# Three pairs of neighbouring RWKV stages, each issued as one, in a hybrid RWKV-7 / attention block

## The chip, the cores and the metric

The kernel runs on one core of a Trainium2 chip. The metric is the device time of one execution in microseconds; the time before is the median of three runs. The work is spread over TensorE (PE, with its weight loads shown as PEld), VectorE (DVE), ScalarE (ACT), GpSimd (POOL) and SyncE (SP), which issues the transfers.

## The reference

One decoder block in fp32: 16 learned meta tokens are put ahead of 256 tokens, a projection feeds two branches (RWKV-7 time mixing and an attention with forget gates, "FoX"; 16 heads of 64 each), a gated merge joins them, and a SwiGLU network follows. The part that the change touches is the time mixing:

```python
def step(S, inp):
    r_t, w_t, k_t, v_t, a_t, b_t = inp
    sa = jnp.einsum('bhvk,bhk->bhv', S, a_t)
    S = (S * w_t[:, :, None, :] + sa[..., None] * b_t[:, :, None, :]
         + v_t[..., None] * k_t[:, :, None, :])
    return S, jnp.einsum('bhvk,bhk->bhv', S, r_t)
...
y = _wkv7_scan(rh, dh, kh, vh, -kk, kk * ah)
y = (y - mu) * lax.rsqrt(var + GN_EPS)
y = y * gn_w + gn_b
y = y + jnp.sum(rh * kh * r_k, axis=-1, keepdims=True) * vh
```

## The kernel before

**Weights.** Each product with a weight matrix is made of three TensorE passes: the weight tile `raw` comes by a transfer, ACT casts its high part `wh` (L336), DVE subtracts to get the low part `wl` (L337), and TensorE multiplies high by high, high by low and low by high (L347 to L349; L423 and L425 where the two activations stand side by side). raw, wh and wl have four buffers each, so ACT and DVE run at most four tiles ahead of TensorE.

**Groups.** The 16 heads are worked in four groups g of four heads. For each group TensorE runs jobs over weight tiles: RWKV k, v and r, two low-rank products, FoX q, k and v (with f for the attention's k), and behind groups 0 to 2 two gate jobs (zg). Behind group 3 come nine more gate jobs, then the branch products, the output product and the SwiGLU network.

**Background streams.** What is not a weight product is a generator: `rwkv_bg` for time mixing and `fox_bg` for attention. It issues one stage and yields a number, in ns of a virtual clock, after which the next stage may come. The jobs call `slot` after every k-tile, which moves the virtual clock on and issues the stages that are due. The order of TensorE is what this gives at build time, and TensorE works strictly down that list. The other engines' order is chosen by a scheduler from the same program. The names Y_* are the yielded numbers.

**The time mixing of one group**, in stages of `rwkv_bg`: norms and decays (to Y_AB); first tables, m = 0, then second tables, m = 1 (L782 to L787: 16 small fp32 matmuls `mat` each by L373, evicted into NK by DVE L786); the meta block's tables (8 matmuls, DVE L795) with the transfers d1 and ln; bonus bs (L829); two transposes trbk of the bk tables (L842, ACT L843); the values' transposes trv (ACT L852); the meta block's transposes tr0 (ACT L859 and L861). Then DVE eliminates in 31 steps (lt L874, lx L876), in 112 lanes. The result goes through DRAM into X and X0 by 13 transfers of SP (d2 L881, d3 L883, X L887, X0 L888). After a yield of LANE = 24000 the chain begins: XT is transposed on DVE (L953) while TensorE makes rhs of the meta block, then QT (32 tiny matmuls, evicted by ACT L962), X12 (evicted by ACT L970), four scan steps (rhs, u, y, s), a group norm on DVE (L979 to L988, its reciprocal root in L263 to L272) and the transposes yT back to channel order (L996, put into ya by L999 to L1005). A group's chain runs while TensorE does the next group's jobs, so a group's norm and its yT fall among the next group's tables. FoX stages wait in `slot` for a chain stage to share a place with, as far as the four small PSUM banks allow.

Words used below: a main matmul is one of L347 to L349; an island is a run of small matmuls between two main ones; sc are FoX's scores, fss and fk its norms' sums.

Of the kernel before, what the change touches and what calls it, by code (L numbers as in the profile page):

```python
# [81 lines left out]
Y_KK = 2900  # L82
Y_DECAY = 1400
Y_AB = 6000
Y_MAT = 2900
Y_NEXT = 2300
Y_BONUS = 1200
Y_TRBK = 1400
Y_TRV = 1100
Y_TR0 = 1600  # L90
Y_RHS = 1400
Y_U = 1400
Y_XT = 1400
# [7 lines left out]
def hybrid_block(ctx, tc, A, out, dbg=None):  # L101
# [18 lines left out]
    def aux_ps(name):  # L120
        return psa.tile([P, 512], F32, tag="aux", name=name)
# [249 lines left out]
    def pe_mm(out_, lhsT, rhs, start, stop, skip=False):  # L371
        clock[2] += 4 * max(lhsT.shape[-1], rhs.free_size()) / 2.4
        nc.tensor.matmul(out_, lhsT, rhs, start=start, stop=stop, skip_group_check=skip)  # L373

    def pe_tr(out_, in_, ident_):
        clock[2] += P / 2.4
        nc.tensor.transpose(out_, in_, ident_)
# [278 lines left out]
    def rwkv_jobs(g):  # L656
# [24 lines left out]
        def mul(w):  # L681
            (uh, ul), (gh, gl) = w
            gg = box["gg"] = ot(f"gg{g}")
            for m in range(2):
                ms = slice(m * P, (m + 1) * P)
                ps = main_ps(f"g{g}{m}")[:, :T]
                for k in range(2):
                    mm3(ps, gh[:, k, ms], gl[:, k, ms], sgh[:, k, :], sgl[:, k, :], k == 0, k == 1)
                nc.vector.tensor_copy(gg[:, m, :], ps)
            with tc.manual_schedule(engines={nc.scalar.engine}):  # L690
                for nm, i, dh, dl, bname in (("sig", 0, twh, twl, "w0"), ("aa", 1, adh, adl, "a0")):
                    dst = box[nm] = et(f"{nm}{g}")
                    for m in range(2):
                        ms = slice(m * P, (m + 1) * P)
                        ps = (aux_ps if i == 0 else main_ps)(f"{nm}{g}{m}")[:, :L]
                        mm3(ps, uh[:, i, ms], ul[:, i, ms], dh, dl, True, True)
                        nc.scalar.activation(dst[:, m, :], ps, AF.Sigmoid, bias=vc(bname, 2 * g + m))

                nc.scalar.preload_act_table_set("natural_log_exp_and_others")
            spawn(rwkv_bg(g, box), HOP)  # L700
# [3 lines left out]
    def hb(h):  # L704
        return slice(h * HD, (h + 1) * HD)

    def tok(c):

        return slice(0, HD) if c < 0 else slice(NMETA + c * HD, NMETA + (c + 1) * HD)

    def bcast(ap, n):
        return ap.unsqueeze(1).to_broadcast([P, n, ap.shape[1]])

    def rwkv_bg(g, box):
# [64 lines left out]
        for m in range(2):  # L779
            pss = [aux_ps(f"mat{g}{m}{h}") for h in range(2)]  # L780
            for c in range(4):
                for h in range(2):  # L782
                    pe_mm(pss[h][:, c * P:(c + 1) * P], bk[hb(h), m, c].rearrange("p x t -> p (x t)"),
                                     ar[hb(h), :, m, tok(c)], start=True, stop=True)
            for h in range(2):
                nc.vector.tensor_tensor(NK[:, h, 4 * m:4 * m + 4, :], pss[h].rearrange("p (c w) -> p c w", w=P),  # L786
                                        bcast(mup, 4), op=ALU.mult)  # L787
            yield Y_MAT
        pss = [aux_ps(f"mat0{g}{h}") for h in range(2)]
        for m in range(2):  # L790
            for h in range(2):
# [47 lines left out]
        for m in range(2):  # L839
            ps = aux_ps(f"trbk{g}{m}")  # L840
            for c in range(4):
                pe_tr(ps[:, c * P:(c + 1) * P], bkf[:, 4 * m + c, :], ident)  # L842
            nc.scalar.activation(BK[:, :, 4 * m:4 * m + 4, :].rearrange("p h c d -> p c h d"),  # L843
                                 ps.rearrange("p (c h d) -> p c h d", h=2, d=HD), AF.Copy)
            yield Y_TRBK
        ps = aux_ps(f"trv{g}")
        for m in range(2):
            for e in range(2):
# [2 lines left out]
        for cc in range(2):  # L851
            nc.scalar.activation(SV[HD:, :, cc::2, :].rearrange("p h i d -> p i h d"),  # L852
                                 ps[hb(cc), :].rearrange("p (i h d) -> p i h d", h=2, d=HD), AF.Copy)
        yield Y_TRV
        ps = aux_ps(f"tr0{g}")
        for m in range(2):
            pe_tr(ps[:, m * P:(m + 1) * P], bk0[:, m].rearrange("p x t -> p (x t)"), ident)
# [4 lines left out]
                             ps[:NMETA, 2 * P:].rearrange("p (m h d) -> p m h d", h=2, d=HD), AF.Copy)  # L862
        yield Y_TR0

# [578 lines left out]
```

## Time and profile before

| | us |
|---|---|
| runs | 1537.67, 1539.15, 1539.01 (median 1539.01) |
| profiled execution | 1540.85 |
| its span, mean granted clock | 1539.1, 0.999 |
| PE busy | 1529.6 (99%) |
| DVE busy | 1030.4 (67%) |
| ACT busy | 778.2 (51%) |
| POOL busy | 106.8 (7%) |
| waits of PE in the trace | 0.2 to 2.0 in an entry, six entries |

The groups' time mixing and attention lie in about the first 560 us of the span; the rest is gates, branches and the SwiGLU network. Busy shares over the whole span mix these, so the stages around one group's elimination are read in windows of their own. Times in timeline rows are from the span's start.

### The profile page before, as it was taken

What the parts mean: (1) busy time and instruction counts of PE and PEld (TensorE: products, weight loads), DVE (VectorE), ACT (ScalarE), POOL (GpSimd) and SP (SyncE); (2) the same over time, 40 slices, a digit from 0 to 9 for tenths busy, and PEclk for the clock granted to TensorE, in tenths of its full rate; (3) what the DMA queues carried; (4) which work ended last, traced back from release to release, by engine and by line L of the source; (5) the groups of instructions that cost most, each with busy time, mean ns of one, the idle gap of its engine ahead of it and who ended that gap; (6) DMA issues with size and microseconds to landing.
All of it is one profiled execution on the core that took longest, in us unless ns stands there. A gap on an engine that the chain in (4) does not pass through costs nothing.

```text
span 1539.1 us, 25987 instructions
## 1 busy us (share of the span) xinstructions
PE 1529.6 (99%) x10113; PEld 1352.5 (88%) x10113; DVE 1030.4 (67%) x1859; ACT 778.2 (51%) x1174; POOL 106.8 (7%) x186
## 2 busy tenths in 40 slices
PE   9999999999999999999999999999999999999998
PEld 9999899989989888998888888888888888888887
DVE  7887698688788857876565566666556666444443
ACT  7654465475465445554455455445445544333332
POOL 2111203302202000000000000000000000000000
PEclk9999999999999999999999999999999999999999
DMA  8566546546645757777566666666666665566663
GB/s 269 163 171 185 148 134 188 163 119 188 175 125 154 212 155 218 230 226 240 181 180 185 192 185 186 191 192 182 189 191 191 182 190 189 191 204 204 189 203 104
DMA packets 211483, 283.32 MB, mean 184 GB/s; under 512 B 23888, under 2 KB 128352, under 8 KB 211360
## 3 DMA queue, kind: packets, MB, share of 16 engines
q1 hardware_dynamic: 206752, 277.53, 60.7%
q10 hardware_dynamic: 4608, 4.13, 0.8%
q8 instruction: 79, 1.29, 0.3%
q14 instruction: 44, 0.36, 0.1%
HBM read 274.43 MB, written 7.19 MB: 183 GB/s over the span
## 4 chain that ended last, share of the span: by engine, by line
PE 95%; DVE 2%; ACT 1%; DMA 1%; SPq 1%; issue 1%; DVEq 0%; ACTq 0%
PE up L423 11%; PE gt L423 10%; PE zg L423 8%; PE dn L1306 5%; PE dn L1305 5%; PE dn L1304 5%; PE up L425 5%; PE gt L425 5%; PE zg L425 4%; PE f L347 2%; PE f L349 2%; PE f L348 2%; PE br L347 2%; PE f L423 2%; PE br L348 2%; PE br L349 2%
## 5 line engine op out<-in xcount | busy, mean ns | idle before, releaser
L337 DVE TENSOR_TENSOR wl<-raw,wh 128x1024 fp32r<-128x1024 f32 (+1 forms) x376 | 456.7, 1216 | 264.0 <-ACT wh L336 263.4
L336 ACT ACTIVATE wh<-raw 128x1024 fp32r<-128x1024 f32 (+1 forms) x376 | 393.9, 1049 | 424.8 <-PE up L423 117.5
L318 DVE TENSOR_TENSOR wl<-raw,wh 128x1024 fp32r<-128x1024 f32 x120 | 147.0, 1225 | 162.8 <-ACT wh L317 162.7
L423 PE MATMUL gt<-hts,wh 128*128 128x512 f32 x704 | 245.0, 394 | 0.0
L423 PE MATMUL up<-hts,wh 128*128 128x512 f32 x704 | 244.9, 394 | 0.0
L317 ACT ACTIVATE wh<-raw 128x1024 fp32r<-128x1024 f32 x120 | 127.0, 1058 | 194.4 <-PE dn L1305 141.5
L425 PE MATMUL gt<-hts,wl 128*128 128x256 f32 x660 | 186.2, 282 | 0.0
L425 PE MATMUL up<-hts,wl 128*128 128x256 f32 x660 | 186.0, 282 | 0.0
L423 PE MATMUL zg<-xhl,wh 128*128 128x512 f32 x512 | 182.4, 401 | 0.0
L423 PEld LDWEIGHTS up<-hts,wh 128*128 128x128 f32 x704 | 130.1, 188 | 26.5
L423 PEld LDWEIGHTS gt<-hts,wh 128*128 128x128 f32 x704 | 130.1, 188 | 26.5
L1305 PE MATMUL dn<-wh,acl 128*128 128x512 f32 x352 | 138.7, 394 | 0.0
L1306 PE MATMUL dn<-wl,ach 128*128 128x512 f32 x352 | 138.3, 393 | 0.0
L1304 PE MATMUL dn<-wh,ach 128*128 128x512 f32 x352 | 138.1, 392 | 0.0
L425 PE MATMUL zg<-xhl,wl 128*128 128x256 f32 x480 | 135.0, 281 | 0.0
L425 PEld LDWEIGHTS up<-hts,wl 128*128 128x128 f32 x660 | 124.7, 189 | 1.8
L425 PEld LDWEIGHTS gt<-hts,wl 128*128 128x128 f32 x660 | 124.7, 189 | 1.8
L423 PEld LDWEIGHTS zg<-xhl,wh 128*128 128x128 f32 x512 | 94.3, 188 | 19.4 <-issue 0.7
L425 PEld LDWEIGHTS zg<-xhl,wl 128*128 128x128 f32 x480 | 90.6, 189 | 1.2
L1304 PEld LDWEIGHTS dn<-wh,ach 128*128 128x128 f32 x352 | 66.0, 188 | 15.7
L1305 PEld LDWEIGHTS dn<-wh,acl 128*128 128x128 f32 x352 | 66.1, 188 | 15.4
L1306 PEld LDWEIGHTS dn<-wl,ach 128*128 128x128 f32 x352 | 66.1, 188 | 14.7
(464 smaller groups left out, 2937.9 us busy)
## 6 DMA issues: line engine op xcount, KB each, us to landing
raw<-in_w_gate_up_dram SPq DMA_DIRECT2D x176, 512.0 KB, 3.7
raw<-in_w_in_dram SPq DMA_DIRECT2D x160, 512.0 KB, 4.1
raw<-in_w_down_dram SPq DMA_DIRECT2D x88, 512.0 KB, 4.8
raw<-in_w_o_dram SPq DMA_DIRECT2D x32, 512.0 KB, 4.1
raw<-in_w_branch_a_dram SPq DMA_DIRECT2D x16, 512.0 KB, 4.6
raw<-in_w_branch_b_dram SPq DMA_DIRECT2D x16, 512.0 KB, 4.7
zgd<-zg ACTq DMA_DIRECT2D x30, 128.0 KB, 1.7
gate<-zgd SPq DMA_DIRECT2D x15, 256.0 KB, 6.0
```

The lines of the kernel that those rows point to most:

```text
L317: nc.scalar.activation(th, rr, AF.Copy)
L318: nc.vector.tensor_tensor(tl, rr, th.bitcast(F32), op=ALU.subtract)
L336: nc.scalar.activation(wh[:prow, cs_], raw[:prow, cs_], AF.Copy)
L337: nc.vector.tensor_tensor(wl[:prow, cs_], raw[:prow, cs_], wh[:prow, cs_].bitcast(F32), op=ALU.subtract)
L347: nc.tensor.matmul(ps, wh, ah, start=first, stop=False)
L348: nc.tensor.matmul(ps, wh, al, start=False, stop=False)
L349: nc.tensor.matmul(ps, wl, ah, start=False, stop=last)
L423: nc.tensor.matmul(ps.rearrange("p (a t) -> p a t", a=2), wh, act, start=first, stop=last)
L425: nc.tensor.matmul(ps[:, :T], wl, act[:, 0, :], start=False, stop=False)
L1304: nc.tensor.matmul(o, ah[:, kt, ts_], hi, start=first, stop=False)
L1305: nc.tensor.matmul(o, al[:, kt, ts_], hi, start=False, stop=False)
L1306: nc.tensor.matmul(o, ah[:, kt, ts_], lo_, start=False, stop=last)
```

## The change

The second tables are followed by the meta block's tables without a yield, both trbk transposes are in one stage, and trv and tr0 are in one stage. The yielded numbers are set anew: Y_MAT once 3300 in place of twice 2900, Y_TRBK once 2400 in place of twice 1400, Y_TRV gone, Y_TR0 1800 in place of 1600. No instruction is added or removed.

```diff
-Y_MAT = 2900
+Y_MAT = 3300
 Y_NEXT = 2300
 Y_BONUS = 1200
-Y_TRBK = 1400
-Y_TRV = 1100
-Y_TR0 = 1600
+Y_TRBK = 2400
+Y_TR0 = 1800
...
             for h in range(2):
                 nc.vector.tensor_tensor(NK[:, h, 4 * m:4 * m + 4, :], pss[h].rearrange("p (c w) -> p c w", w=P),
                                         bcast(mup, 4), op=ALU.mult)
-            yield Y_MAT
+            if m == 0:
+                yield Y_MAT
         pss = [aux_ps(f"mat0{g}{h}") for h in range(2)]
...
             nc.scalar.activation(BK[:, :, 4 * m:4 * m + 4, :].rearrange("p h c d -> p c h d"),
                                  ps.rearrange("p (c h d) -> p c h d", h=2, d=HD), AF.Copy)
-            yield Y_TRBK
+        yield Y_TRBK
         ps = aux_ps(f"trv{g}")
...
-        yield Y_TRV
         ps = aux_ps(f"tr0{g}")
```

In the changed kernel's rows a line number can be one lower than before (L372 for L373, L952 for L953).

The first place is on TensorE, at QT of group 1. Before, QT stands at the end of the v job (its row is 1936 of TensorE's list), 15 main matmuls behind the scores sc:

```order
L349 MATMUL v_1_3724<-xhl,wl 128x272
L373 MATMUL QT_3871<-XT_3823,N_3181 32x32 x16
L373 MATMUL u1-1_3890<-R1-1_3831,X_3371 64x64 x4
L347 MATMUL v_1_3724<-xhl,wh 128x272
L348 MATMUL v_1_3724<-xhl,wh 128x272
L349 MATMUL v_1_3724<-xhl,wl 128x272
L347 MATMUL r_0_3916<-xhl,wh 128x258
```

And now (its row is 1893), with the scores behind it:

```order
L348 MATMUL v_0_3723<-xhl,wl 128x272
L372 MATMUL QT_3803<-XT_3772,N_3146 32x32 x16
L372 MATMUL u1-1_3822<-R1-1_3780,X_3310 64x64 x4
L372 MATMUL sc_3830<-kn_2547,qn_2546 128x144
L372 MATMUL sc_3831<-kn_2547,qn_2546 128x144
L372 MATMUL sc_3830<-kn_2547,qn_2546 128x272
L372 MATMUL sc_3831<-kn_2547,qn_2546 128x272
L346 MATMUL v_0_3723<-xhl,wh 128x272
```

QT has moved up past 39 main matmuls and past sc. It is the same in groups 0 and 2; in group 3 the matmuls it passes are 28 of the gates'.

The second place is on TensorE, at yT of group 0, which falls among the tables (mat) of group 1. Before, yT comes behind both tables, the meta tables, fk and the bonus:

```order
L377 MATMUL yT_3238<-ident,Y_2337 128x128 x4
L423 MATMUL zg_0_3258<-xhl,wh 128x512
L425 MATMUL zg_0_3258<-xhl,wl 128x256
L423 MATMUL zg_0_3258<-xhl,wh 128x512
L425 MATMUL zg_0_3258<-xhl,wl 128x256
L377 MATMUL trbk_3269<-ident,bk_2925 128x128 x4
```

Now it comes 30 main matmuls behind the first tables, with the second and the meta tables behind it:

```order
L348 MATMUL f_1_3025<-xhl,wl 128x272
L376 MATMUL yT_3097<-ident,Y_2269 128x128 x4
L346 MATMUL f_1_3025<-xhl,wh 128x272
L347 MATMUL f_1_3025<-xhl,wh 128x272
L348 MATMUL f_1_3025<-xhl,wl 128x272
L372 MATMUL mat_3112<-ar_2931,bk_2934 128x128
L372 MATMUL mat_3113<-ar_2931,bk_2934 128x128
```

It has moved from behind the bonus to ahead of the second tables; the same holds for yT of groups 1 and 2.

The third place is on DVE, around the norm's last instruction (Y times its root) which that yT reads. Before, the second tables' evictions (L786) come straight behind it:

```order
L272 TENSOR_TENSOR s_2987<-gt,s_2987 128x8
L988 TENSOR_TENSOR Y_2337<-Y_2337,s_2987 128x512
L786 TENSOR_TENSOR NK_3035<-mat_3097,mup 128x512
L786 TENSOR_TENSOR NK_3035<-mat_3098,mup 128x512
L1045 SCALAR_TENSOR_TENSOR sqf_2999<-fk_3124,epsw 128x272
```

And now:

```order
L336 TENSOR_TENSOR wl<-raw,wh 128x1024
L270 TENSOR_SCALAR gt<-gt 128x8
L271 TENSOR_TENSOR s_2909<-gt,s_2909 128x8
L987 TENSOR_TENSOR Y_2269<-Y_2269,s_2909 128x512
L1000 COPY ya<-yT_3097 64x4x64 x2
L1002 SCALAR_TENSOR_TENSOR ya<-ya,vcol,bo_1527 128x256 x2
L785 TENSOR_TENSOR NK_3038<-mat_3112,mup 128x512
```

Between the attention norm's last step (L1037) and this instruction stand five weight splits, where four stood before, and yT's evictions (L1000, L1002) come between it and the second tables' evictions.

## The prediction

> **What bounds the kernel now.** I began with the page's busy times and its chain.
>
> ```profile
> PE 1529.6 (99%) x10113; PEld 1352.5 (88%) x10113; DVE 1030.4 (67%) x1859; ACT 778.2 (51%) x1174; POOL 106.8 (7%) x186
> PE 95%; DVE 2%; ACT 1%; DMA 1%; SPq 1%; issue 1%; DVEq 0%; ACTq 0%
> ```
>
> TensorE is busy for 99% of the span and carries 95% of the chain. A change can therefore gain only by shortening TensorE's own list, or by removing one of its few waits. It loses whenever that list, whose order is fixed, reaches an instruction whose input is late. The waits of PE hold one entry that the change touches:
>
> ```profile
> PE X L373 <- ACT QT L962: 2.0, 4, 1.5
> ```
>
> How much room the scan's chain has at the place where it begins is read from the timeline, group 1 first, then the same QT in groups 0, 2 and 3 (start, duration, then the instruction):
>
> ```profile
> 284.95 0.97 PE L373 MATMUL sc<-kn,qn 64*128 64x144 f32 x8
> 285.86 0.39 PE L347 MATMUL v<-xhl,wh 128*128 128x272 f32 x1
> 286.09 0.29 PE L348 MATMUL v<-xhl,wh 128*128 128x272 f32 x1
> 286.22 0.29 PE L349 MATMUL v<-xhl,wl 128*128 128x272 f32 x1
> ...
> 287.93 0.69 PE L373 MATMUL QT<-XT,N 32*32 32x32 f32 x32
> ...
> 162.55 0.63 PE L373 MATMUL QT<-XT,N 32*32 32x32 f32 x28
> 410.30 0.47 PE L373 MATMUL QT<-XT,N 32*32 32x32 f32 x18
> 531.39 0.40 PE L373 MATMUL QT<-XT,N 32*32 32x32 f32 x13
> ```
>
> Main matmuls follow each other every 0.125 us (286.09 to 286.22). QT needs XT, which needs X, which needs the 31 elimination steps on DVE. The windows from the first to the last of these steps, one per group, show what DVE does there (PE, PEld, DVE, ACT, POOL):
>
> ```profile
> 123.90:150.28 26.38, 26.38 (x181) 24.70 (x180) 24.45 (x76) 11.29 (x14) 1.40 (x3) 1.00 0.64 187
> 247.72:273.99 26.27, 26.27 (x178) 24.43 (x177) 24.58 (x76) 10.87 (x13) 3.00 (x6) 1.00 0.65 188
> 370.43:397.87 27.44, 27.44 (x188) 25.61 (x187) 25.55 (x77) 11.73 (x14) 2.98 (x6) 1.00 0.65 192
> 492.12:519.52 27.40, 27.40 (x158) 23.98 (x157) 25.78 (x78) 11.93 (x16) 1.94 (x3) 1.00 0.69 194
> ```
>
> DVE is full in all four (93 to 94%, the rest being steps between dependent small instructions). So the elimination's length is set by how many other instructions stand between its steps, not by TensorE.
>
> **The change part by part.** *Fewer islands.* The second tables and the meta block's tables are fp32 matmuls between main ones. What such an island costs beyond its matmuls shows where one stands alone (y) and where two stand together (u and y):
>
> ```profile
> 216.38 0.29 PE L349 MATMUL f<-xhl,wl 128*128 128x272 f32 x1
> ...
> 216.98 0.40 PE L347 MATMUL f<-xhl,wh 128*128 128x272 f32 x1
> 217.22 0.29 PE L348 MATMUL f<-xhl,wh 128*128 128x272 f32 x1
> ...
> 213.69 0.29 PE L349 MATMUL f<-xhl,wl 128*128 128x272 f32 x1
> ...
> 214.52 0.39 PE L347 MATMUL f<-xhl,wh 128*128 128x272 f32 x1
> 214.75 0.29 PE L348 MATMUL f<-xhl,wh 128*128 128x272 f32 x1
> ```
>
> Alone: 217.22 - 216.38 = 0.84, less two pitches of 0.125, is 0.59 us. Two together: 1.06 - 0.25 = 0.81. Joining saves 2 x 0.59 - 0.81 = 0.37 us, once in each group: -1.5 us. The merged transposes are costed at nothing: they are not fp32 matmul islands of that kind, and four, six or eight of them are still as many of the same instruction; should they behave like the tables, two more joins per group would give -3.0 us (lower bound of this term).
>
> *The chain is issued earlier.* The yields from Y_MAT to Y_TR0 lose 11300 - 7500 = 3800 ns of the virtual clock per group, so LANE ends earlier, and everything of the chain stands earlier among the main matmuls. By TensorE's two orders, 39 main matmuls fewer stand before QT in groups 0 to 2 (in group 3, 28 wider ones of as much time), and the scores sc now come behind QT. That is 39 x 0.125 = 4.9, and 0.91 for sc (284.95 to 285.86): 5.8 us less lead.
>
> X does not come earlier by as much. The first elimination step stands behind the same weight split (wl) as before, and that waits for ACT's cast, which waits for buffers that TensorE frees. Between the first and the last step the new DVE order has more work: a wl is 1.15 (start to start), a z is 0.43, and k, of the same size, is taken like it (the last step of group 1 ends at 273.99):
>
> ```profile
> 273.91 1.23 DVE L337 TENSOR_TENSOR wl<-raw,wh 128x1024 fp32r<-128x1024 f32 x1
> 275.06 0.43 DVE L468 TENSOR_TENSOR z<-k,rsb 128x272 f32<-128x272 f32 x1
> ...
> 281.88 1.23 DVE L337 TENSOR_TENSOR wl<-raw,wh 128x1024 fp32r<-128x1024 f32 x1 [1.39 <-ACT wh L336]
> 283.02 0.44 DVE L953 STREAM_TRANSPOSE XT<-X 128x256 f32<-128x256 f32 x1
> ...
> 159.18 0.45 DVE L953 STREAM_TRANSPOSE XT<-X 128x256 f32<-128x256 f32 x1 [1.09 <-DMA X<-d]
> ```
>
> Group 1 gets two wl, two z and two k: +3.9 us; group 2 one wl and two of each less a rest: +2.4; group 3 a wl and a gate piece: +1.5; group 0 a wl and a z, against a start up to 1.4 earlier: +0.1.
>
> After the last step, X goes through 13 DMAs of SP (the last issue of each group below), then XT. In group 0, XT waited for X, 8.9 us after the last step, 0.7 after the last issue.
>
> ```profile
> 281.14 0.45 SPq L888 DMA_DIRECT2D X<-d  x1
> ...
> 158.47 0.45 SPq L888 DMA_DIRECT2D X<-d  x1
> 405.95 0.45 SPq L888 DMA_DIRECT2D X<-d  x1
> 526.67 0.45 SPq L888 DMA_DIRECT2D X<-d  x1
> ```
>
> With the same 0.7, X is there at 8.9, 7.9, 8.8 and 7.9 us after the last step, and XT adds 0.5. QT could have begun at 159.7, 282.4, 407.2 and 527.9; it began 2.9, 5.5, 3.1 and 3.5 us later. That is the slack. New stall = 5.8 - slack + lateness of the elimination: 5.8 - 2.9 + 0.1 = 3.0; 5.8 - 5.5 + 3.9 = 4.2; 5.8 - 3.1 + 2.4 = 5.1; 5.8 - 3.5 + 1.5 = 3.8. Sum **+16.1 us**. Upper end, with 8.9 in every group, 18 to 20. Lower end: however early X were, XT stands on DVE behind a wl whose cast waits for TensorE to finish the tile before QT (281.88 above waited so), and from that tile's end it is about 2.4 us to XT's end (cast, split, XT); 4 x 2.4 = 9.6. I take 16.1, being built from each group's rows. Behind QT all of TensorE waits, since its list is in order.
>
> *The old wait.* QT's eviction on ACT was late for the X12 matmuls by 2.0 us in all, because ACT's cast ahead of it waited for a weight. With QT late, ACT has no cast left to wait for: -2.0 us (0 if it stays).
>
> *yT moves ahead of the second tables.* In groups 1 to 3 the previous group's yT now stands 30 main matmuls behind the first tables, and the second and meta tables behind yT. It needs L988, the end of the norm's steps on DVE (group 1):
>
> ```profile
> 211.04 0.95 PE L373 MATMUL fss<-bsum,sqf 128*128 128x2 f32 x8
> ...
> 222.98 0.29 PE L349 MATMUL f<-xhl,wl 128*128 128x272 f32 x1
> 223.20 1.16 PE L373 MATMUL mat<-ar,bk 64*128 64x128 f32 x16
> ...
> 224.52 0.29 PE L348 MATMUL f<-xhl,wh 128*128 128x272 f32 x1
> ...
> 237.39 0.60 PE L377 MATMUL yT<-ident,Y 128*128 128x128 f32 x4
> ...
> 212.08 0.35 DVE L1034 TENSOR_SCALAR hs<-fss,eps 128x4 f32<-128x4 f32 x2
> ...
> 229.49 0.69 DVE L988 TENSOR_TENSOR Y<-Y,s 128x512 f32<-128x512 f32 x1
> ```
>
> Before, yT had 7.2 us to spare (230.18 to 237.39). From fss to the first tables it was 12.2 us; in the new order the u, y and y islands (0.81 + 0.59) and three mains have left that stretch: 10.4. The tables take 224.52 - 222.98 - 0.25 = 1.29, and yT comes 1.29 + 30 x 0.125 = 5.0 after they begin, 15.4 after fss, which is 14.4 after L1034. DVE took 18.1 from L1034 to the end of L988 (230.18 - 212.08). I take that less an estimated 0.6, which it spent waiting for TensorE's u: 17.5. Stall 3.1, and 0.4 for the tables and fk behind it, which wait for their evictions: 3.5 x 3 = **+10.5 us**. From below 0.5 each if DVE runs ahead (+1.5), from above 4.3 (+13).
>
> *The clock.* The one long PE wait of before was followed by this (same columns, then granted clock):
>
> ```profile
> 166.83 0.24 PE L373 MATMUL X<-X,QT 32*32 32x32 f32 x2 [1.53 <-ACT QT L962]
> ...
> 169.30:173.00 3.70, 3.70 (x21) 3.70 (x20) 2.37 (x3) 1.15 (x2) 3.45 (x5) 0.54 0.26 55
> ```
>
> A stretch at clock 0.54, of 3.7 us, costs 3.7 x 0.46 = 1.7 us. If a 1.5 us wait brings one, each of four QT waits of 3 to 5 us should; the old one goes: 4 x 1.7 - 1.7 = **+5.1 us**. I put none to yT: its stall may be shorter, and a slow TensorE after it lets DVE catch up (three more windows bound it, +5).
> The Trainium skill, "TensorE: Matmul & The Clock Gate", section "HAM oscillation — how this bites in real kernels", speaks against this change too: it calls idle gaps of TensorE over some 3.4 us the ones after which the clock halves. By that rule only the three QT waits above that length would cost a window, 3 x 1.7 - 1.7 = +3.4 in place of +5.1. This trace does not bear the limit out, since 0.54 followed a wait of 1.53 us.
>
> **Sum**: 16.1 + 10.5 + 5.1 - 2.0 - 1.5 = +28.2 on the profiled execution's 1540.85 (span 1539.1), 1569.0. The median of the runs, 1539.01, is 1.8 below that execution: **1567 us**.
>
> **The rivals.** *yT is hidden* (25%): DVE runs ahead while TensorE stands at QT, so L988 is done in time. For it: yT had 7.2 us before. Against: the 18 us from L1034 to L988 hold five wl in the new order, four in the old. 28.2 - 10.5 = +17.7: 1557. *The clock stays up* (12%): waits do not halve it, and 0.54 had another cause; +23.1: 1562. *Only the floor is paid* (10%): X keeps up with the chain, only XT's place behind its wl costs; 9.6 - 3.5, no yT: +6: 1545.
>
> *The other side: faster* (8%). The first elimination step starts earlier by as much as the chain, because what holds its wl is not TensorE but ACT's evictions of trv, which now come sooner. This row, just ahead of group 1's first step, has such a wait:
>
> ```profile
> 246.58 1.22 DVE L337 TENSOR_TENSOR wl<-raw,wh 128x1024 fp32r<-128x1024 f32 x1 [1.47 <-ACT wh L336]
> ```
>
> Then only the savings stay: -2.0 - 1.5 = -3.5, 1535.5. It decides if the start moves by at least the stalls above, 3 to 5 us; the wait shown has 1.5 to give, which is why it is unlikely.
>
> **How the numbers follow.** Forecast 45% at 1567 (its own range 1558 to 1579). The low end, floors for both waits and no new slow windows, is 9.6 + 1.5 - 3.5 = +7.6, 1547; the high end 20 + 13 + 5.1 + 5 - 3.5 = +39.6, 1579. So 1547 to 1579. The clock, yT and half of the floor cases are in it. A measurement here tells 0.2%, 3 us, from no change. Faster 0.05 and same 0.04 share the last rival and mixtures with the floor; slower 0.91.
>
> **What would show it.** Right: PE's waits list QT behind DVE's XT with some 16 us in four, and yT behind L988 with 9 us in three; windows of clock near 0.5 follow them; the two-table island costs 0.37 less than its parts. Wrong: XT ending before QT's place with PE never idle, the elimination's first step moving ahead of its old wl, or a window of 250 to 275 us in which DVE has idle time.

## The result

The changed kernel takes 1580.25 us (median of 4 runs, 1578.78 to 1581.37) against 1538.59 us for the one before, measured beside it: 1.0271 times as long, 95% interval 1.0258 to 1.0284. It is slower, as forecast, by 41.7 us where 28 were forecast, and 1.25 us above the top of the range. The profiled executions are 1581.37 and 1540.85 us, 40.5 apart.

The page's busy line and the granted clock of the changed kernel, to set beside 1529.6 and 0.999:

```profile
PE 1542.0 (98%) x10113; PEld 1362.1 (86%) x10113; DVE 1027.4 (65%) x1859; ACT 779.6 (49%) x1174; POOL 99.1 (6%) x186
...
core 0: 1579.7 us, clock 0.989
```

TensorE has the same 10113 matmuls and is busy 12.4 us longer, so nearly a third of the loss is time in which it worked slowly; the rest is time in which it stood. The waits of PE in the changed kernel (total us, how often, the longest):

```profile
PE QT L372 <- DVE XT L952: 20.3, 4, 6.4
PE yT L376 <- DVE Y L987: 5.2, 3, 2.1
PE f L348 <- DVE wl L336: 2.4, 3, 0.8
...
PE fk L636 <- DVE NK L785: 0.9, 2, 0.4
PE s L372 <- DVE sv L919: 0.7, 3, 0.4
...
PE mat L372 <- ACT ya L998: 0.4, 2, 0.2
```

The entry X12 <- QT (2.0 us before) is gone. QT's four waits and yT's three, from the timeline:

```profile
160.49 0.34 PE L372 MATMUL QT<-XT,N 32*32 32x32 f32 x5 [3.07 <-DVE XT L952]
295.57 0.34 PE L372 MATMUL QT<-XT,N 32*32 32x32 f32 x5 [5.79 <-DVE XT L952]
430.42 0.28 PE L372 MATMUL QT<-XT,N 32*32 32x32 f32 x3 [6.37 <-DVE XT L952]
563.19 0.32 PE L372 MATMUL QT<-XT,N 32*32 32x32 f32 x5 [5.02 <-DVE XT L952]
...
234.45 0.30 PE L376 MATMUL yT<-ident,Y 128*128 128x128 f32 x1 [1.57 <-DVE Y L987]
368.38 0.30 PE L376 MATMUL yT<-ident,Y 128*128 128x128 f32 x1 [2.08 <-DVE Y L987]
503.44 0.30 PE L376 MATMUL yT<-ident,Y 128*128 128x128 f32 x1 [1.56 <-DVE Y L987]
```

The windows in which the clock was halved (length, PE busy, matmuls, clock), all five that there were within the span:

```profile
160.45:167.28 6.83, 6.79 (x78) 0.50 0.79 234
293.57:300.40 6.83, 4.83 (x55) 0.50 0.58 159
368.67:372.08 3.41, 3.41 (x31) 0.50 0.47 144
426.69:436.93 10.24, 6.51 (x67) 0.50 0.42 114
563.23:570.05 6.82, 6.82 (x82) 0.50 0.57 172
```

One belongs to each QT wait (in groups 1 and 2 it begins inside the wait, in groups 0 and 3 at its end), and one follows the longest yT wait. Counted at half speed, half of the 28.4 us that TensorE was busy in them is lost, 14.2 us; before it was half of one such stretch of 3.41, 1.7. The difference is 12.5 us. This is an estimate, and rather high: in the stretch of before, main matmuls of 258 columns followed each other every 0.215 us, and behind it every 0.12.

How late X was: the windows of the elimination in groups 1 to 3, and in group 1 the two groups of DVE instructions that differ most from before (the last two rows are the kernel before, in the window of its own group 1):

```profile
255.86:286.88 31.02, 31.02 (x217) 29.24 (x216) 27.57 (x82) 12.88 (x15) 1.60 (x4) 1.00 0.64 188
390.03:421.64 31.61, 31.61 (x223) 29.67 (x223) 27.67 (x82) 12.77 (x15) 1.60 (x4) 1.00 0.63 184
524.75:554.78 30.03, 30.03 (x173) 26.32 (x172) 26.14 (x80) 13.53 (x17) 0.00 (x0) 1.00 0.69 202
...
L336 DVE TENSOR_TENSOR wl<-raw,wh 128x1024 fp32r<-128x1024 f32 x12 | 14.7, 1228 | 1.7 <-ACT wh L335 1.7
...
L429 DVE TENSOR_TENSOR zg<-zg,zg 128x256 f32<-128x256 f32 x4 | 1.7, 417 | 2.0 <-ACT zg L428 2.0
...
L337 DVE TENSOR_TENSOR wl<-raw,wh 128x1024 fp32r<-128x1024 f32 x10 | 12.2, 1221 | 1.5 <-ACT wh L336 1.5
...
L430 DVE TENSOR_TENSOR zg<-zg,zg 128x256 f32<-128x256 f32 x4 | 1.7, 414 | 0.0
```

The elimination takes 31.0, 31.6 and 30.0 us, 4.8, 4.2 and 2.6 longer than before. In group 1 two wl more than before are 2.4 us of it (12 and 10 in the rows, which count the one ahead of the first step and the one behind the last; 10 and 8 between the steps), and two z and two k, which were not there before, are 1.9. DVE also stood 2.0 us inside it for a gate piece: it waited for ACT, and ACT for TensorE's gate job.

### The profile page after: what moved, and what is told of

It is laid out like the page before. It is cut to its first block, busy times and chain, and to the rows that moved or that the text cites. A ratio compares the mean times of both kernels' runs of the same rounds, so it can differ in the third digit from the quotient of the medians.

```text
span 1579.7 us, 25992 instructions
## 1 busy us (share of the span) xinstructions
PE 1542.0 (98%) x10113; PEld 1362.1 (86%) x10113; DVE 1027.4 (65%) x1859; ACT 779.6 (49%) x1174; POOL 99.1 (6%) x186
## 3 DMA queue, kind: packets, MB, share of 16 engines
q8 instruction: 79, 1.29, 0.3%
## 4 chain that ended last, share of the span: by engine, by line
PE 82%; DVE 4%; SPq 1%; DMA 1%; issue 1%; POOL 0%; ACT 0%; DVEq 0%; ACTq 0%; POOLq 0%
PE up L422 10%; PE gt L422 10%; PE zg L422 6%; PE dn L1305 5%; PE dn L1304 5%; PE dn L1303 5%; PE up L424 5%; PE gt L424 5%; PE zg L424 3%; PE br L346 2%; PE br L347 2%; PE br L348 2%; PE wo L1305 2%; PE wo L1304 2%; PE wo L1303 2%; PE f L422 1%
```

## The experiments

Two theories: the loss comes from the chain's earlier place in TensorE's list (the virtual clock lost 3.8 us); or from the merged stages themselves.

**1. The merges stay, the chain goes back.**

```diff
-LANE = 24000
+LANE = 27800
```

> The change with the chain put back by one number, LANE = 27800 for 24000: the merged stages stay, and QT stands 6 to 3 main matmuls from where it stood before the change. If the loss is the chain's earlier place (TensorE reaching QT and yT before their inputs, then running at half clock), no wait of QT or yT is left and the time is that of before less the joined islands, 1535 to 1538 us. If the merged stages themselves hold TensorE up, it stays above 1550 us.

Measured: 1539.05 us, 1.0002 times before [0.9994, 1.0011], 1 us above the expected range. Its waits of PE that are not before's, and its clock:

```profile
PE tr L376 <- ACT sv L852: 1.3, 1, 1.3
...
PE trbk L376 <- ACT bt L843: 0.7, 1, 0.7
PE tr L376 <- ACT ya L998: 0.6, 1, 0.6
...
core 0: 1537.4 us, clock 1.000
```

One number undoes the whole loss, so the merges alone do not cost it. The waits at QT, yT and X12 and the half clock are gone. The joined tables save what was forecast; here they are in group 0 (24 matmuls, 102.65 to 104.42):

```profile
102.65 0.29 PE L348 MATMUL f<-xhl,wl 128*128 128x272 f32 x1
102.87 1.39 PE L372 MATMUL mat<-ar,bk 64*128 64x128 f32 x24
...
104.42 0.29 PE L347 MATMUL f<-xhl,wh 128*128 128x272 f32 x1
```

1.77 - 0.25 = 1.52 us in place of 1.29 + 0.59 = 1.88. New waits of 2.6 us at the merged transposes, for ACT's evictions, are more than the 1.5 us that the four joins save.

**2. No merge, the chain early.**

```diff
-LANE = 24000
+LANE = 20200
```

(in the kernel before)

> The kernel before with LANE = 20200 for 24000 and no stage merged: the chain is issued 3.8 us of the virtual clock earlier, QT stands 33 to 36 main matmuls earlier. If the earlier place is the cause: QT waits of 17 to 20 us in all, yT (now between the second and the meta tables) waits 3 to 6 us, clock at half after them for 10 to 14 us of loss, 1570 to 1580 us. If merging is the cause: 1538 to 1550 us.

Measured: 1550.82 us, 1.0080 [1.0066, 1.0094]. The time lies outside both ranges: 19 us below the first theory's, 0.8 us above the second's.

```profile
PE QT L373 <- DVE XT L953: 4.9, 4, 1.9
PE f L349 <- DVE wl L337: 2.4, 3, 0.8
PE s L373 <- DVE sv L920: 2.2, 2, 1.2
```

The early place alone costs 12 us. The elimination is 26.1, 26.0 and 26.3 us long in groups 1 to 3, not 30 to 31.6, and yT, here behind the second tables but ahead of the meta tables, does not wait. So neither theory holds alone: early and merged together cost 41.7, early alone 12, merged alone nothing. One thing that differs is the length of the elimination; runs 4 to 6 follow it up.

**3. Keep TensorE busy while it waits.** Extra matmuls into QT's own PSUM tile, which QT then overwrites; the waits stay.

```diff
         ps = aux_ps(f"QT{g}")
+        for _ in range((20, 40, 44, 34)[g]):
+            nc.tensor.matmul(ps[:, :L], bones, xh[:, 0, :], start=True, stop=True)
```

> The change with idle-time matmuls: right ahead of QT, TensorE does 20, 40, 44 and 34 extra 128x272 matmuls (groups 0 to 3) whose result is overwritten, 0.125 us each, 17.3 us in all, in the 20.3 us in which it waited for XT. If the wait itself brings the half clock, the four windows after QT go and the time falls by some 12.5 us to 1566 to 1570 us. If the half clock comes from the tiny matmuls of QT and X12 and not from the idle time, the time stays at 1577 to 1582 us. If it comes from both, in between.

Measured: 1572.86 us, 1.0222 [1.0208, 1.0236], 7.4 us less than the change.

```profile
PE QT L372 <- DVE XT L952: 2.8, 4, 1.2
PE s L372 <- DVE sv L919: 2.7, 3, 1.7
...
core 0: 1570.3 us, clock 0.998
```

```profile
290.00:297.00 7.00, 5.75 (x78) 1.00 0.32 78
```

With TensorE busy, the clock stays at 1.00 around QT in all four groups (group 1 shown), though the small matmuls of QT and X12 are the same: the half clock at QT does not come without the wait. Fillers (138 x 0.125 = 17.3) and rest (2.8) are as long as the waits were (20.3). The time, though, is between the two ranges. The profiled execution is 9.4 us shorter than the changed kernel's, not 12.5: s now waits 2.0 us more, and one half-clock stretch, behind that wait, took the place of the one behind yT. The other 1.1 us are not accounted for.

**4. yT later.** To tell what yT's place does.

```diff
-NORM = 6500
+NORM = 11500
```

> The change with NORM = 11500 for 6500: yT stands behind the second tables, fk and bonus again (21 main matmuls behind bonus), QT stays early. By the waits of PE in the changed kernel, yT, fk, the tables and the v/f weights behind them lose 8.9 us in groups 1 to 3 and one half-clock stretch 1.7: at least 10.6 less, 1569.6. The DVE order also has two wl, two z and two k less among the elimination's steps of groups 1 and 2: if the elimination's length sets X, the QT waits fall from 20.3 to 9 to 13 us too and the time is 1556 to 1563; if the QT waits do not depend on it, 1568 to 1571.

Measured: 1556.47 us, 1.0113 [1.0098, 1.0129]. QT stands as early as with the change, yet waits only 6.0 us in all, less than the 9 to 13 expected, and there is no wait of yT; the time is in the range of the theory that the elimination's length sets X. The 2.4 us at f for wl are still there, as in run 2: they belong to the early place and not to yT.

**5. yT by 12 main matmuls later.** A small step, which takes it just behind the second tables.

```diff
-NORM = 6500
+NORM = 7000
```

> The change with NORM = 7000 for 6500: yT stands 12 main matmuls behind the second tables, where the change has it 3 ahead of them; QT stands within 3 main matmuls of the change's place. DVE's list has 9 wl instead of 11 among the elimination's steps of groups 1 and 2, and no z or k. If yT's place ahead of the tables matters by DVE's list (the elimination 31 us long for 26), the QT waits fall from 20.3 to 5 to 8 us and the time to 1553 to 1560 us. If yT costs only what TensorE itself waits at it, 1568 to 1573 us.

Measured: 1556.57 us, 1.0119 [1.0103, 1.0134]. 23.7 us of the 41.7 hang on whether yT stands 3 main matmuls ahead of the second tables or 12 behind them. PE's waits, and the elimination in groups 1 and 2:

```profile
PE QT L372 <- DVE XT L952: 5.3, 2, 3.1
...
252.94:278.07 25.13, 25.13 (x169) 23.35 (x168) 23.45 (x76) 10.86 (x13) 0.00 (x0) 1.00 0.66 192
378.31:403.43 25.12, 25.12 (x169) 23.32 (x168) 23.44 (x76) 10.86 (x13) 0.00 (x0) 1.00 0.68 192
```

The elimination is 25.1 us, 6 less, with 8 wl between its steps in place of 10 and no z or k. QT's waits go from 20.3 to 5.3; in groups 1 and 2 there is none. Otherwise TensorE's list differs from the changed kernel's only by single islands that stand a few main matmuls earlier or later.

**6. Both cases in one run.** Only the tables merged, the chain as early as with the change; yT stands ahead of the second tables in groups 1 and 3, behind them in group 2.

```diff
-LANE = 24000
+LANE = 22700
...
+            if m == 0:
+                yield Y_MAT
```

> Only the tables merged, LANE = 22700, so that the chain stands as early as with the change (QT within 3 main matmuls). In group 1 and 3 yT stands 3 main matmuls ahead of the second tables and DVE's list has 10 wl among the elimination's steps; in group 2 yT stands 12 behind them and there are 8. If the list of DVE sets the QT waits, they are long in groups 1 and 3 (4 to 7 us) and short in group 2 (0 to 2 us), in one run; if the merged transposes matter, all are short; if only the early place matters, all are alike. Time 1562 to 1570 by the first.

Measured: 1565.53 us, 1.0175 [1.0161, 1.0188]. QT in groups 0 to 3, and the elimination in groups 1 to 3:

```profile
158.50 0.28 PE L373 MATMUL QT<-XT,N 32*32 32x32 f32 x7 [2.99 <-DVE XT L954]
291.52 0.28 PE L373 MATMUL QT<-XT,N 32*32 32x32 f32 x3 [5.47 <-DVE XT L954]
417.76 0.31 PE L373 MATMUL QT<-XT,N 32*32 32x32 f32 x9 [1.13 <-DVE XT L954]
548.61 0.32 PE L373 MATMUL QT<-XT,N 32*32 32x32 f32 x4 [4.21 <-DVE XT L954]
```

```profile
251.76:282.81 31.05, 31.05 (x218) 29.26 (x217) 27.60 (x82) 12.88 (x15) 1.60 (x4) 1.00 0.62 187
382.59:407.70 25.11, 25.11 (x169) 23.34 (x168) 23.43 (x76) 10.86 (x13) 0.00 (x0) 1.00 0.68 199
510.63:540.34 29.71, 29.71 (x171) 26.04 (x170) 26.08 (x80) 13.52 (x17) 0.00 (x0) 1.00 0.71 204
```

Groups 1 and 3 have the long elimination and the long waits, group 2 neither, in one execution. (Group 0, ahead of which no yT stands, waits as with the change.) The merged transposes are not needed for it. In this run DVE has 10 wl between the elimination's steps where yT stands ahead of the second tables, and 8 where it does not. Why the scheduler does so, no run shows, and yT's place is not the only way to it: in run 12, where yT stands far behind, group 1 has 10 wl too and takes 28.6 us.

**7 and 8. Each merge alone, the chain late.** 7 merges only the tables, 8 only the transposes.

```diff
-LANE = 24000
+LANE = 26500
```

```diff
-LANE = 24000
+LANE = 25300
```

> Only the tables merged, the chain where it was (LANE = 26500). The joined islands save 4 x 0.37 = 1.5 us, and the 2.0 us wait at X12 with its half-clock stretch may go as it did with all three merges and LANE = 27800: 1534 to 1538 us. If the joining saves nothing, 1538 to 1540.

Measured (7): 1540.46 us, 1.0012 [1.0003, 1.0021], a miss: X12's wait went (0.2 left), but a wait of 1.9 us at s in group 1, with a half-clock stretch behind it, took its place.

> Only the transposes merged, the chain where it was (LANE = 25300). With all three merges and the chain put back, TensorE waited 2.6 us at tr and trbk for ACT's evictions; if those belong to the merged transposes, they are here too and the time is 1537 to 1542; if they come with the tables, none, 1535 to 1538.

Measured (8): 1544.73 us, 1.0036 [1.0023, 1.0049], a miss too: 0.7 us at trbk, none at tr, and 3.4 us at X12 in group 2 (for DVE's SV), again with a half-clock stretch.

**9 to 12. Other places.** Four ways to keep the tables' saving, or none, and take the chain off its waits: 9 all merges and LANE = 29800; 10 tables only and 27500; 11 tables and trbk, with trv and tr0 as two stages, and 27900; 12 the kernel before with 25500.

> All three merges with LANE = 29800: QT stands 12 to 21 main matmuls later than before the change. The joined tables save 1.5 us. If the waits of some 2 us that were left with LANE = 27800 (at tr) are a matter of the chain's place against ACT's list, they change with it: 1535 to 1541 us, faster than before by 0.2% only if no wait over 1 us and no half clock is left.

> Only the tables merged, LANE = 27500: QT stands 2 to 15 main matmuls later than before the change, 2 to 9 later than with LANE = 26500, whose profile had a wait of 1.9 us at s in group 1 and a half-clock stretch behind it. If that wait is a matter of the place, it is gone: 1535 to 1538 us; if the merged tables bring it, it stays: 1539 to 1541.

> Tables and trbk merged, trv and tr0 as two stages again, LANE = 27900. The 1.9 us that TensorE waited at tr for ACT's evictions of trv, with all three merged and LANE = 27800, go if the merge of trv and tr0 brings them: 1534 to 1537 us. If they come from the place, there are others: 1537 to 1541.

> The kernel before with LANE = 25500 and no merge: QT 9 to 15 main matmuls later. The X12 wait of 2.0 us and its half-clock stretch of 1.7 us may go as a matter of place; no island is saved. 1535 to 1539 us; by DVE's list the elimination of group 1 and 3 has 2 and 1 wl more among its steps, but QT has room for it.

| run | us | against before |
|---|---|---|
| 9 | 1551.13 | 1.0081 [1.0069, 1.0094] |
| 10 | 1545.53 | 1.0040 [1.0027, 1.0053] |
| 11 | 1542.32 | 1.0017 [1.0008, 1.0026] |
| 12 | 1552.14 | 1.0081 [1.0068, 1.0093] |

None is faster, and all four lie above their expected ranges. The rows of 12 that take the most:

```profile
PE s0-1_2320 L373 <- DVE SV L920: 2.9, 1, 2.9
PE s2-1_5654 L373 <- DVE SV L920: 2.0, 1, 2.0
```

Moving the chain later does not free it: its scan steps then wait for DVE's copies, 0.5 to 2.9 us each in the four runs, and half-clock stretches follow in 9, 10 and 12. Run 11 has no wait at tr, where 1 and 9, with trv and tr0 merged, have 1.9 and 2.6 us; run 8 has that merge too and no wait, so the merge alone does not bring them. No version found beats the kernel before; with all merges and the chain back (run 1) it is equal.

## Why the prediction was right or wrong

The direction and the mechanism held: QT is ahead of its X, yT ahead of its norm, TensorE stands, and the clock drops. Two sizes were too small, the clock's above all. Term by term (us):

| term | forecast | measured |
|---|---|---|
| QT's waits | +16.1 | +20.3 |
| yT, and the tables and fk behind it | +10.5 | +6.5 (5.2 + 0.9 + 0.4) |
| half clock | +5.1 | +12.5, an estimate |
| X12's wait | -2.0 | -2.0 |
| joined tables | -1.5 | -1.5 (4 x 0.36, rows of run 1) |
| f for wl, s for sv | none | +3.1 |
| sum | +28.2 | +38.9 |

1.6 us of the 40.5 between the profiled executions are left over. The joined tables are taken from run 1; in the changed kernel itself the joined island cost 1.52 us in group 0 as well, but 2.05 in groups 1 and 3, 0.22 of it a wait that is in the second row. That is 0.6 of the 1.6; the rest stays open.

- **The clock** is the term that failed: +5.1 was forecast, some +12.5 came. The forecast took one half-clock stretch for each QT wait, 1.7 us, from the only one that the trace had. With waits of 3 to 6 us the clock stayed low for two or three windows of 3.41 us, and the loss was some 14.2 us in five stretches. That the waits bring it was right, as run 3 shows; that the clock might stay up was the rival, and it fell. Giving none to yT was nearly right: one of its three waits had one.
- **QT's waits.** Group by group 3.1, 5.8, 6.4 and 5.0 against 3.0, 4.2, 5.1 and 3.8. Lead and slack were right to within some 0.7 us: the same sum with the measured lateness gives 5.1, 6.9 and 4.9 for groups 1 to 3. Right, too, was XT waiting for X and not for its wl (the floor case fell: in group 1 DVE stood idle before XT, for X, for 3.7 us, in the changed kernel's timeline). The lateness of the elimination was too small: 3.9, 2.4 and 1.5 were forecast for groups 1 to 3, and 4.8, 4.2 and 2.6 came. It was made of instruction times alone. The instructions were counted rightly (two, one and one wl more), but DVE's own wait inside the elimination, for zg, was not counted, since DVE was full there before: it was 2.0, 2.1 and 2.1 us.
- **yT.** 1.6 to 2.1 us each in place of 3.1. By the changed kernel's timeline TensorE's 14.4 was the one that was off: it took 15.6 us in all three groups, 0.8 of it its own wait at f for wl, which the forecast did not have. DVE took 17.0, 17.5 and 17.0 where 17.5 was forecast. So part of what yT did not cost is in the row of f.
- **Not seen**: that yT's place, 3 main matmuls ahead of the second tables, goes with the long elimination. The prediction took the two as separate terms; run 5 shows that with yT 12 main matmuls later the elimination loses 6 us and the whole 23.7, and run 6 has both cases side by side. It read both lists and used the additional wl, but did not ask what they depend on.
- **The rivals.** yT was not hidden. Faster fell: the first step of the elimination did not move ahead of its old wl (in group 1 it stands behind 82 of them in both traces). The sum of the high ends, 1579, was 1.25 us short although yT came 6.5 below its own high end: the clock cost 2.4 more than its bound of one window per wait (5.1 + 5), f and s cost 3.1 that no term had, QT cost 0.3 more than its 20, and 1.6 is left over.
- **The Trainium skill**, "TensorE: Matmul & The Clock Gate", section "HAM oscillation — how this bites in real kernels", puts the half clock behind idle gaps of over some 3.4 us, and the three QT waits above that (5.79, 6.37 and 5.02) agree with it. As a limit it does not hold here: 2.08 and 3.07 us brought the half clock too, 1.57 did not. What decides is closer to how much of a wait falls into one window, as the last section shows.

## What to carry to other kernels

When a list in fixed order is issued earlier, the gain of a few tenths of a us in the list is set against each input's slack; read the slack of every consumer that moves up, and of what feeds it on the other engines, from the trace. A yield is also a delay: taking it out moves all that follows, so merge stages and give the time back in one place before judging the merge. In a kernel like this one, where TensorE is 99% busy, count 1.7 to 3.4 us more for the clock with a wait of 3 to 6 us: that is what the half-clock stretches behind such waits cost in these runs, by the same estimate.

## What the runs showed of the hardware that was not expected

The half clock comes in windows of 3.41 us: each stretch above is one, two or three of them (3.41, 6.83, 10.24). What a window brings goes with how long TensorE was busy in it. In the traces of all runs, behind the first 10 us, every window at full clock with less than 1.67 of 3.41 us busy was followed by half clock, and none with more than 2.35. So the length of a wait alone does not tell: 1.9 us in one window of run 9 (1.51 us busy) brought the half clock, 2.0 us spread over two windows of run 12 (2.35 and 2.47 busy) did not.

Between these bounds both occur, and the busy share alone does not decide. Two windows of the kernel before and one of run 11, each with the one that follows it:

```profile
43.02:46.43 3.41, 2.31 (x18) 1.00 0.73 217
46.43:49.84 3.41, 3.41 (x29) 1.00 0.16 52
165.90:169.31 3.41, 2.32 (x49) 1.00 0.95 317
169.31:172.72 3.41, 3.41 (x19) 0.50 0.20 35
...
288.74:292.15 3.41, 2.30 (x51) 1.00 0.67 215
292.15:295.57 3.42, 3.42 (x37) 1.00 0.53 153
```

With the same 2.3 us busy, the first, with 18 main matmuls, was followed by full clock; the second, where most of the 49 were the small ones of X12 and s, by half clock. That small matmuls count for less than their time would be a reading of this pair, but the third window, of run 11, holds the same mixture of small and main ones and was followed by full clock. What decides between the bounds stays open; run 3 shows that the small ones alone, without the wait, do not bring the half clock.
